# Low fp16 halves of attention weights on GpSimd: every second 512 columns of the long rows, one Trainium2 core

## Chip, cores and metric

The kernel runs on 1 core of one Trainium2 chip. The metric is the device time of one execution in microseconds (us). Before the change the median of 3 runs is 2537.69 us (2535.66 to 2538.88). Engines are named as in the profile: PE is TensorE's matmuls and PEld its weight loads, DVE is VectorE, ACT is ScalarE, POOL is GpSimd, SP is SyncE, whose queue issues the DMAs.

## What is computed

One inference step of a one-layer streaming encoder: an input projection, a short causal convolution, differential attention on 4 heads, an output projection, an MLP and a gated embedding. The attention is what the change touches:

```
u = RMSNorm(h);  z = u @ W_in -> [B | C | X | Q | K | V]
s = einsum('bqhmd,bkhmd->bhmqk', q, k) * HEAD_DIM**-0.5 - slope_h * |t - s|     # two maps m = 0, 1
s = where(chunk(k) <= chunk(q), s, -1e30)
a = softmax(s);  attn = a[:, :, 0] - lam * a[:, :, 1]
o = attn @ v;  o = RMSNorm(o) * (1 - lambda_init)
```

2048 prompt tokens, 64-token chunks, queries in blocks of 128.

## The kernel before

Nearly every matmul is made of three fp16 matmuls: an operand is scaled and split into a high half hi (fp16 of the scaled value) and a low half lo (the scaled value minus hi), and hi*hi, hi*lo and lo*hi are summed in PSUM. `split` (L168) does that with two instructions: ACT writes hi (L170), then DVE writes lo with one scalar_tensor_tensor (L105, through the helper `stt`). `split_in_place` (L173) is another form, used late in the kernel: the source is scaled in place, ACT rounds it to hi, and GpSimd subtracts.

The stages, by the trace: normalised input and first projections (to about 150 us), attention with the other projections woven in (about 150 to 900 us), then the output projection and the MLP's two matrix products, then the embedding gate. The change lies in attention.

Attention goes head by head (j = 0 to 3), and in a head by query blocks of 128 rows; `Unit` is one block. Block qb sees nk = (qb + 1) * 128 keys, taken in pieces of up to 512 columns (`self.chunks`). In heads 0 to 2 qb runs from 0 to 15, in head 3 from 15 down to 0. A unit passes three steps, and `weave` interleaves the steps of three successive units with "fill", generators of projection matmuls and other small work:

- `scores`: two matmuls per piece and map (L617, L618), then on DVE a fused scale, bias and running maximum from PSUM into the fp32 tile s (L621). After the last piece POOL negates the maximum (nm, L100) and ACT takes the exponential of the whole row in place and sums it (L629).
- `weigh` and `turn`, one unit later: POOL and DVE make the two factors r and sg from the row sums. Per piece DVE adds the two maps (L646, into map 0's tile s1), `split` turns the sum into hi and lo, which lie side by side as fp16 in map 1's tile s2 (L647, L648), and one DMA on SP's queue transposes both (L657) into a tile at.
- `values`, another unit later: three 128-column matmuls per 128 keys (L667 to L669) sum into one of four slots of a PSUM tile smb. `subnorm` (L515) then squares the slot on ACT (jko, L518), makes a factor on POOL (rso) and scales on DVE (yg); this also frees the slot.

There are 16 units per head. The units of heads 0 to 2 and the first nine of head 3 (qb 15 to 7) go this way (`by_dma`); the last seven of head 3 use `turn_and_values`, which the change leaves alone. While head 3 ends, `early` splits the output projection's weights (w<-wst, four scaled by i_wo and four by aswo) and starts the first tiles of that projection (L959 to L963).

The order on each engine is fixed when the program is built: a scheduler places the instructions of all engines by their dependencies and its own estimates, in about the order in which they were written. At run time each engine works through its list in that order. SP's DMAs do too. Tile s has four buffers, so two units have rows in flight, and a row's tile is reused when all its readers are done.

Of the kernel before, what the change touches and what calls it, by code (L numbers as in the profile page):

```python
# [11 lines left out]
AF = mybir.ActivationFunctionType  # L12
# [22 lines left out]
def hymba_step_kernel(  # L35
# [9 lines left out]
    V, A, G, T = nc.vector, nc.scalar, nc.gpsimd, nc.tensor  # L45
# [58 lines left out]
    def stt(out, a, s1, b, op0, op1):  # L104
        V.scalar_tensor_tensor(out=out, in0=a, scalar=s1, in1=b, op0=op0, op1=op1)  # L105

    MUL, ADD, SUB, MAX = ALU.mult, ALU.add, ALU.subtract, ALU.max
# [60 lines left out]
    def split(hi, lo, src, scale):  # L168

        A.activation(out=hi, in_=src, func=AF.Copy, scale=scale)  # L170
        stt(lo, src, scale, hi, MUL, SUB)
# [421 lines left out]
    class Unit:  # L593
# [46 lines left out]
        def turn(self):  # L640

            s1, s2 = self.s
            self.ats = []
            for i, (c0, w_) in enumerate(self.chunks):
                cs = slice(c0, c0 + w_)
                stt(s1[:, cs], s2[:, cs], self.r, s1[:, cs], MUL, ADD)  # L646
                hl = s2[:, cs].bitcast(F16)  # L647
                split(hl[:, :w_], hl[:, w_:], s1[:, cs], self.sg)  # L648
                if i < 2 or self.even:
                    if i % 2 == 0:  # L650
                        two = pmix.tile([P, 2, NH, 2, P], F16, tag="q4", bufs=3, name="at2")
                    at = two[:, i % 2].rearrange("p a b c -> p (a b) c")
                else:
                    at = att.tile([P, 2, TG], F16, tag="at", bufs=3, name="at")
                    at = at.rearrange("p a (b c) -> p (a b) c", c=P)
                n = w_ // P
                nc.sync.dma_start_transpose(out=at[:, :2 * n, :], in_=hl)  # L657
                self.ats.append((c0, w_, at[:, :n, :], at[:, n:2 * n, :]))
                yield
# [1127 lines left out]
    for n, (m, p, b) in enumerate(BLOCKS):  # L1787
# [15 lines left out]
        if m == M4 and (p, b) > (0, 1):  # L1803
            i = (4 * p + b - 2) * 2
# [46 lines left out]
```

## Time and profile before

| What | Value |
|---|---|
| Median of 3 runs | 2537.69 us (2535.66 to 2538.88) |
| Profiled execution, its own time | 2533.34 us |
| Its span, first to last instruction | 2531.6 us |
| PE busy | 2456.3 us (97%), 15981 matmuls |
| DVE busy | 1692.4 us (67%), 2931 instructions |
| ACT busy | 1139.1 us (45%) |
| POOL busy | 756.0 us (30%) |
| Mean granted TensorE clock | 0.991 |

Busy shares are averages over stages with different limits, so each stage is read by itself. Matmuls overlap and their ends are modelled, so a busy PE is not a PE at its peak. A wait is put down to what released it last. Idle time on an engine matters only where something else waits for that engine.

### The profile page before, as it was taken

To read this page: it belongs to the slowest core of one execution; us is meant where nothing else is said; L and a number is where in the kernel's file an instruction comes from. 1 tells how busy PE (TensorE), PEld (TensorE's weight loads), DVE (VectorE), ACT (ScalarE), POOL (GpSimd) and SP (SyncE) were. 2 spreads that over 40 slices of the span, in tenths; PEclk is the share of its full clock that TensorE was granted. 3 is DMA by queue.
4 is the path that set the end of the run, shared out by engine and by line. 5 is a ranking of instruction groups with operands and counts; after the bars stand their busy time and mean duration, and the time that the engine had idled before them with its cause. 6 is when DMAs were issued, how large, how long until landed. Compare 5 with 4: busy or idle time off the path is not lost.

```text
span 2531.6 us, 41709 instructions
## 1 busy us (share of the span) xinstructions
PE 2456.3 (97%) x15981; PEld 1283.6 (51%) x15981; DVE 1692.4 (67%) x2931; ACT 1139.1 (45%) x1977; POOL 756.0 (30%) x1307
## 2 busy tenths in 40 slices
PE   8999999999999799999999999999999999999998
PEld 7756655755745444444444444444444444444444
DVE  7578978969988857866665665654455547646664
ACT  5436635635643645643443443454233223425553
POOL 2143344334333434422222222210121102314442
PEclk9999999999999799999999999999999999999999
DMA  5134534524544335454444444366554547631221
GB/s 181 52 84 96 103 81 89 117 61 103 123 104 107 87 120 162 165 209 164 167 160 158 158 175 137 129 243 219 197 193 148 175 152 248 214 96 60 79 84 55
DMA packets 345083, 345.35 MB, mean 136 GB/s; under 512 B 150473, under 2 KB 241042, under 8 KB 344882
## 3 DMA queue, kind: packets, MB, share of 16 engines
q1 hardware_dynamic: 344882, 342.68, 44.4%
q8 instruction: 125, 2.05, 0.3%
q14 instruction: 76, 0.62, 0.1%
HBM read 206.68 MB, written 97.92 MB: 120 GB/s over the span
## 4 chain that ended last, share of the span: by engine, by line
PE 79%; DVE 9%; DMA 5%; ACT 3%; issue 3%; POOL 2%; SPq 0%; DVEq 0%; POOLq 0%; ACTq 0%
PE mm L1383 8%; PE mm L1385 8%; PE mm L1384 8%; PE mm L1614 7%; PE mm L1616 7%; PE mm L1615 7%; PE mm L959 4%; PE mm L961 4%; PE mm L963 4%; PE lin L317 4%; PE lin L318 4%; PE lin L319 4%; DVE s L105 2%; DVE s L621 2%; PE sc L617 1%
## 5 line engine op out<-in xcount | busy, mean ns | idle before, releaser
L1616 PE MATMUL mm<-v,hl 128*128 128x512 f16 x896 | 339.8, 380 | 3.1 <-DVE hl L1576 3.1
L1614 PE MATMUL mm<-v,hl 128*128 128x512 f16 x896 | 339.3, 380 | 2.1 <-ACT hl L1575 2.0
L1615 PE MATMUL mm<-v,hl 128*128 128x512 f16 x896 | 340.3, 380 | 0.0
L317 PE MATMUL lin<-uh,whl 128*128 128x512 f16 (+1 forms) x832 | 261.6, 330 | 4.1 <-DVE yt L105 1.3
L318 PE MATMUL lin<-ul,whl 128*128 128x512 f16 (+1 forms) x832 | 262.2, 330 | 0.7 <-DVE ul L105 0.7
L1576 DVE TENSOR_TENSOR hl<-fr,hl 128x1024 f16<-128x1024 f32 x112 | 150.0, 1349 | 168.1 <-ACT hl L1575 167.2
L319 PE MATMUL lin<-uh,whl 128*128 128x512 f16 (+1 forms) x832 | 261.7, 330 | 0.7 <-DVE whl L105 0.7
L1575 ACT ACTIVATE hl<-fr 128x1024 f16<-128x1024 f32 x112 | 116.7, 1051 | 301.7 <-PE mm L1616 278.2
L629 ACT ACTIVATE s<-s,nm 128x128 f32<-128x128 f32 (+15 forms) x128 | 153.5, 1199 | 167.1 <-POOL nm L100 166.4
L1383 PE MATMUL mm<-u,w 128*128 128x512 f16 x448 | 169.8, 379 | 1.1 <-ACT w L170 1.1
L1384 PE MATMUL mm<-u,w 128*128 128x512 f16 x448 | 169.8, 379 | 0.0
L1384 PE MATMUL mm<-u2b,w 128*128 128x512 f16 x448 | 169.8, 379 | 0.0
L1383 PE MATMUL mm<-u2b,w 128*128 128x512 f16 x448 | 169.2, 379 | 0.5 <-DMA u2b<-u_d 0.5
L1385 PE MATMUL mm<-u,w 128*128 128x512 f16 x448 | 168.8, 379 | 0.0
L1385 PE MATMUL mm<-u2b,w 128*128 128x512 f16 x448 | 168.5, 379 | 0.0
L621 DVE CUSTOM_DVE_ANT_0 s<-sc,bias,mx 128x512 f32<-128x512 f32 (+3 forms) x192 | 134.9, 702 | 16.0 <-PE sc L618 11.8
L1614 PEld LDWEIGHTS <-hl 128*128 128x128 f16 x896 | 87.8, 98 | 112.2 <-issue 6.9
L1616 PEld LDWEIGHTS <-hl 128*128 128x128 f16 x896 | 87.7, 98 | 110.7 <-DVE hl L1576 4.9
L1385 PEld LDWEIGHTS <-w 128*128 128x128 f16 x896 | 87.7, 98 | 105.3
L1615 PEld LDWEIGHTS <-hl 128*128 128x128 f16 x896 | 87.7, 98 | 104.5 <-issue 1.5
L1383 PEld LDWEIGHTS <-w 128*128 128x128 f16 x896 | 88.7, 99 | 100.2 <-ACT w L170 1.2
L1384 PEld LDWEIGHTS <-w 128*128 128x128 f16 x896 | 87.7, 98 | 99.2 <-issue 0.8
(464 smaller groups left out, 5847.8 us busy)
## 6 DMA issues: line engine op xcount, KB each, us to landing
ff_d<-e SPq DMA_DIRECT2D x224, 256.0 KB, 2.1
fr<-ff_d SPq DMA_DIRECT2D x112, 512.0 KB, 4.5
raw<-in_w_down_dram SPq DMA_DIRECT2D x80, 512.0 KB, 4.7
xt<-in_x_prompt_dram SPq DMA_DIRECT2D x32, 512.0 KB, 4.4
stg<-in_w_up_dram SPq DMA_DIRECT2D x16, 1024.0 KB, 6.5
stgd<-in_w_down_dram SPq DMA_DIRECT2D x16, 1024.0 KB, 5.6
stg<-in_w_in_dram SPq DMA_DIRECT2D x24, 512.0 KB, 5.3
h_d<-ht SPq DMA_DIRECT2D x16, 512.0 KB, 2.9
```

Source lines behind the costliest of these rows:

```text
L317: T.matmul(o, w[:, 0, ft], rh[:, ft, c], start=(ft == 0), stop=False)
L318: T.matmul(o, w[:, 0, ft], rl[:, ft, c], start=False, stop=False)
L319: T.matmul(o, w[:, 1, ft], rh[:, ft, c], start=False, stop=(ft == FT - 1))
L621: ev = V.tensor_tensor_reduce(out=s_[:, c0:c0 + w_], in0=ps[:, :w_], in1=bias[:, b0:b0 + w_], scale=h["idd"], scalar=-BIG if prev is None ...
L629: A.activation(out=s_[:, :nk], in_=s_[:, :nk], func=AF.Exp, bias=nm, accum_out=zz)
L1383: T.matmul(o, w[:, c, 0, kt], x[:, :, 0, kt], start=first and kt == 0, stop=False, skip_group_check=True)
L1384: T.matmul(o, w[:, c, 0, kt], x[:, :, 1, kt], start=False, stop=False, skip_group_check=True)
L1385: T.matmul(o, w[:, c, 1, kt], x[:, :, 0, kt], start=False, stop=kt == 3, skip_group_check=True)
L1576: V.tensor_tensor(out=hl[:, 1], in0=fr, in1=hl[:, 0], op=SUB)
L1614: T.matmul(ps, hl[:, 0, u % 2, c], v[:, 0], start=(u == 0), stop=False)
L1615: T.matmul(ps, hl[:, 0, u % 2, c], v[:, 1], start=False, stop=False)
L1616: T.matmul(ps, hl[:, 1, u % 2, c], v[:, 0], start=False, stop=(u == NU - 1))
```

## The change

In `turn`, for the pieces with odd index (i = 1 and 3) of the blocks with qb > 7, `split` is replaced by three instructions: ACT multiplies the sum by sg in place, ACT copies it to hi, and GpSimd subtracts hi from the scaled sum into lo. Other pieces and blocks keep `split`.

```diff
                 stt(s1[:, cs], s2[:, cs], self.r, s1[:, cs], MUL, ADD)
                 hl = s2[:, cs].bitcast(F16)
-                split(hl[:, :w_], hl[:, w_:], s1[:, cs], self.sg)
+                if i % 2 and self.qb > 7:
+                    A.activation(out=s1[:, cs], in_=s1[:, cs], func=AF.Copy, scale=self.sg)
+                    A.copy(hl[:, :w_], s1[:, cs])
+                    G.tensor_tensor(out=hl[:, w_:], in0=s1[:, cs], in1=hl[:, :w_], op=SUB)
+                else:
+                    split(hl[:, :w_], hl[:, w_:], s1[:, cs], self.sg)
```

Per head the odd pieces are: i = 1 with 512 columns in the eight blocks qb 8 to 15, and i = 3 in qb 12 to 15 with 128, 256, 384 and 512 columns. That is 12 pieces a head and 48 in all, 36 of 512 columns and 4 each of 384, 256 and 128. In the changed program the three new instructions are lines L649 (scale), L650 (copy, printed as CAST) and L651 (subtract).

The scheduler's order moves with them. In the lists below s_N are row tiles (N is the tile's number, which differs between the two programs), sc the PSUM scores, mx a running maximum, sgc, sg, ca, kk and rz the small factors of a unit.

On DVE, in head 0, the row with qb 12, around the low halves of its pieces. Before:

```order
L621 ISA s_4076,mx<-sc,bias,idd_1557 128x512
L621 ISA mx 128x1
L105 SCALAR_TENSOR_TENSOR s_3847<-s_3786,sg,s_3847 128x512
L140 TENSOR_REDUCE am<-stg 128x1
L105 SCALAR_TENSOR_TENSOR s_3847<-s_3786,sg,s_3847 128x512 x2
L105 SCALAR_TENSOR_TENSOR s_3847<-s_3786,sg,s_3847 128x128
L621 ISA s_4076,mx<-sc,bias,mx,idd_1557 128x512
L621 ISA mx 128x1
```

and now:

```order
L105 SCALAR_TENSOR_TENSOR s_3850<-s_3789,sg,s_3850 128x512
L100 TENSOR_SCALAR yg<-smb,rso 128x128
L105 SCALAR_TENSOR_TENSOR s_3850<-s_3789,sg,s_3850 128x512
L621 ISA s_4080,mx<-sc,bias,mx,idd_1557 128x512
L621 ISA mx 128x1
L621 ISA s_4080,mx<-sc,bias,mx,idd_1557 128x512
L621 ISA mx 128x1
```

The low halves of pieces 1 and 3 are gone from DVE's list; those of pieces 0 and 2 stay, and behind them stand steps of the scores of a later row.

On POOL, at the same row of head 0. Before:

```order
L102 TENSOR_SCALAR rso<-sso,kk 128x1
L102 TENSOR_SCALAR kk<-sg,z_3808,k_0_1759 128x1
L521 TENSOR_TENSOR rso<-rso,mhalf 128x1
L102 TENSOR_SCALAR kk<-kk 128x1
L100 TENSOR_SCALAR nm<-mx 128x1 x2
L102 TENSOR_SCALAR ca<-z_4037,alam,z_4134 128x1
```

and now:

```order
L102 TENSOR_SCALAR rso<-sso,kk 128x1
L521 TENSOR_TENSOR rso<-rso,mhalf 128x1
L100 TENSOR_SCALAR nm<-mx 128x1
L651 TENSOR_TENSOR s_3850<-s_3789,s_3850 128x512
L651 TENSOR_TENSOR s_3850<-s_3789,s_3850 128x128
L100 TENSOR_SCALAR nm<-mx 128x1
L102 TENSOR_SCALAR ca<-z_4041,alam,z_4138 128x1
```

Two subtractions now stand between two negated maxima (nm), and the second nm follows both.

On ACT, near the end of head 3, at the splitting of the output projection's weights. Before:

```order
L170 ACTIVATE yhl<-pty,gsa 128x4x128
L170 ACTIVATE w<-wst,i_wo 128x1024 x4
L629 ACTIVATE s_12357,z_12369<-s_12357,nm 128x1024
L170 ACTIVATE w<-wst,aswo 128x1024 x4
L518 ACTIVATE jko,sso<-smb 128x128
L170 ACTIVATE s_12282<-s_12250,sg 128x512 x2
L170 ACTIVATE s_12282<-s_12250,sg 128x128
L629 ACTIVATE s_12372,z_12396<-s_12372,nm 128x1024
```

and now:

```order
L170 ACTIVATE yhl<-pty,gsa 128x4x128
L170 ACTIVATE w<-wst,i_wo 128x1024 x4
L170 ACTIVATE w<-wst,aswo 128x1024 x4
L629 ACTIVATE s_12404,z_12416<-s_12404,nm 128x1024
L170 ACTIVATE s_12328<-s_12296,sg 128x512
L649 ACTIVATE s_12296<-s_12296,sg 128x512
L170 ACTIVATE s_12328<-s_12296,sg 128x128
L518 ACTIVATE jko,sso<-smb 128x128
L629 ACTIVATE s_12419,z_12443<-s_12419,nm 128x1024
```

The exponential of the row with qb 7 has moved behind all eight weight halves, and jko now follows the three instructions that turn pieces 0 to 2 of the row with qb 8, where it stood ahead of that row's pieces; the copy of its piece 1 comes after the last row shown.

## Rows read from the trace of the kernel before

**Rows 1.** Windows by stage: us, busy us (instructions) per engine, granted clock, DMA share, GB/s.
```profile
150.00:820.00 670.00, 649.01 (x5416) 388.79 (x5415) 564.92 (x1370) 346.01 (x647) 269.04 (x607) 1.00 0.45 98
820.00:900.00 80.00, 60.45 (x396) 35.80 (x395) 61.78 (x144) 48.75 (x105) 36.55 (x95) 0.83 0.33 85
...
1030.00:1650.00 620.00, 618.34 (x3570) 288.32 (x3569) 390.62 (x562) 263.07 (x437) 170.21 (x170) 1.00 0.47 162
```

**Rows 2.** Windows of the four long-row stretches, same columns, with their sum.
```profile
222.00:322.00 100.00, 96.33 (x1041) 67.52 (x1040) 89.86 (x221) 60.68 (x107) 39.40 (x85) 1.00 0.53 110
412.00:502.00 90.00, 86.21 (x943) 62.37 (x943) 81.55 (x193) 59.22 (x107) 33.96 (x75) 0.98 0.54 109
612.00:700.00 88.00, 82.20 (x905) 58.50 (x903) 80.99 (x191) 56.10 (x95) 28.65 (x63) 1.00 0.55 117
700.00:826.00 126.00, 118.21 (x812) 62.27 (x810) 104.65 (x246) 54.46 (x91) 44.68 (x85) 0.99 0.45 104
sum 404.00, PE 382.95 PEld 250.66 DVE 357.04 ACT 230.46 POOL 146.69; mean PE 95.74 PEld 62.66 DVE 89.26 ACT 57.61 POOL 36.67
```

**Rows 3.** Waits of PE, 150 to 820 us: total us, times, longest.
```profile
PE smb L667 <- DMA at<-s: 6.5, 9, 1.1
PE sc L617 <- DVE mx L621: 5.5, 10, 1.0
```

**Rows 4.** Groups of DVE, 150 to 820 us: shapes, count | busy us, mean ns | idle.
```profile
L105 DVE SCALAR_TENSOR_TENSOR s<-s,sg,s 128x512 f16<-128x512 f32 x102 | 73.1, 741 | 6.8 <-ACT s L170 6.7
...
L105 DVE SCALAR_TENSOR_TENSOR s<-s,sg,s 128x384 f16<-128x384 f32 x14 | 8.5, 608 | 1.6 <-ACT s L170 1.6
...
L105 DVE SCALAR_TENSOR_TENSOR s<-s,sg,s 128x256 f16<-128x256 f32 x13 | 6.2, 477 | 1.2 <-ACT s L170 1.2
...
L105 DVE SCALAR_TENSOR_TENSOR s<-s,sg,s 128x128 f16<-128x128 f32 x13 | 4.5, 343 | 0.0
```

**Rows 5.** Groups of ACT, 150 to 820 us, same columns.
```profile
L170 ACT ACTIVATE s<-s,sg 128x512 f16<-128x512 f32 x102 | 68.5, 714 | 61.7 <-DVE s L105 38.0 <-POOL sg L102 21.9 <-POOL kk L102 1.3
```

**Rows 6.** Groups of POOL, 1030 to 1650 us, same columns.
```profile
L1274 POOL TENSOR_TENSOR stg<-stg 128x512 f32<-128x512 f32 x16 | 28.0, 1749 | 14.1 <-DVE w L105 14.1
...
L1267 POOL TENSOR_TENSOR s3t<-stg 128x512 f32<-128x512 f32 x15 | 19.1, 1271 | 141.7 <-DMA stg<-in_w_up_dram 141.7
```

**Rows 7.** Line L105, a DVE helper: min/median/max ns, first and last start, forms.
```profile
L105 DVE SCALAR_TENSOR_TENSOR w<-stg,i_u,w x96: 734/741/1767, 1033.3 to 1637.5; 128x512 f16<-128x512 f32 x96
...
L105 DVE SCALAR_TENSOR_TENSOR e<-mm,sr,e x64: 733/744/753, 1076.8 to 1678.7; 128x512 f32<-128x512 f32 x64
```

**Rows 8.** Timelines of POOL, then DVE, 1632 to 1635 us: start, us, instruction.
```profile
1632.61 1.79 POOL L1274 TENSOR_TENSOR stg<-stg 128x512 f32<-128x512 f32 x1
...
1633.18 1.75 DVE L105 SCALAR_TENSOR_TENSOR w<-s3t,i_u,w 128x512 f16<-128x512 f32 x1
1634.86 0.74 DVE L105 SCALAR_TENSOR_TENSOR w<-stg,i_u,w 128x512 f16<-128x512 f32 x1
```

**Rows 9.** Line L657, the transposing DMAs: min/median/max ns, first and last start.
```profile
L657 SPq DMA_TRANSPOSE at<-s x150: 1181/1258/2643, 156.4 to 849.1; - x150
```

**Rows 10.** Waits of all engines, 150 to 820 us.
```profile
ACT s L629 <- POOL nm L100: 151.2, 70, 6.3
```

**Rows 11.** Timelines of ACT, then PE, around 830 to 842 us.
```profile
830.01 4.26 ACT L170 ACTIVATE w<-wst,i_wo 128x1024 f16<-128x1024 f32 x4 [0.42 <-DVE i_wo L102]
834.18 1.13 ACT L629 ACTIVATE s<-s,nm 128x1024 f32<-128x1024 f32 x1
...
835.31 4.25 ACT L170 ACTIVATE w<-wst,aswo 128x1024 f16<-128x1024 f32 x4
839.47 0.26 ACT L518 ACTIVATE jko<-smb 128x128 f16<-128x128 f32 x1
...
839.72 1.62 ACT L170 ACTIVATE s<-s,sg 128x512 f16<-128x512 f32 x3
...
841.53 0.27 PE L667 MATMUL smb<-vhl,at 128*128 128x128 f16 x1 [6.04 <-DVE yg L100]
```

## The prediction

> **What bounds the kernel now.** I read the windows by stage first. From 150 to 820 us, where attention runs with fill, PE is busy 649.01 of 670 us, DVE 564.92, ACT 346.01 and POOL 269.04; in the MLP stretch from 1030 to 1650 us PE is busy 618.34 of 620 [rows 1]. So attention is bound by PE with DVE close behind, and POOL and ACT have room. At its end, 820 to 900 us, PE is busy only 60.45 of 80 us at a granted clock of 0.83 [rows 1]: the fill is used up, and a chain through the engines sets the pace.
>
> Then I cut out the parts that hold the changed rows, which are four long-row stretches. Together they last 404 us; PE is busy 382.95 and DVE 357.04, that is 88% [rows 2]. PE's idle time there is 404 - 382.95 = 21.05 us. This is all that an easier DVE could give back in these stretches, since the matmuls stay the same. The list of PE's waits says for what it stands: from 150 to 820 us 6.5 us in 9 waits for the transposed weights at, and 5.5 us in 10 waits for a score buffer that DVE must empty [rows 3]. Both can come from a late DVE, but no wait is longer than 1.1 us.
>
> **What leaves DVE.** 48 low halves go: 36 of 512 columns at 741 ns, and 4 each of 384, 256 and 128 columns at 608, 477 and 343 ns [rows 4]. That is 36 * 0.741 + 4 * (0.608 + 0.477 + 0.343) = 26.7 + 5.7 = 32.4 us, 9% of DVE's 357.04 us.
>
> **What POOL's subtraction gives back to DVE.** A subtraction of 512 columns in fp32 takes POOL 1271 ns in one group and 1749 ns in another [rows 6]. The difference is in what DVE does at the same moment. In the timeline POOL's subtraction runs from 1632.61 for 1.79 us; DVE's low half, which reads two SBUF tiles, starts inside it and takes 1.75 us, while the next one, behind it, takes 0.74 [rows 8]. The same form ranges from 734 to 1767 ns over that stage, but one that has a PSUM operand stays between 733 and 753 [rows 7]. So a subtraction can cost a DVE instruction with two SBUF tiles 1.75 - 0.74 = 1.01 us, more than the 0.741 us it saved, and those with a PSUM operand nothing.
>
> How often they meet isn't in the trace of before. By the order on DVE, the score steps that follow the low halves of pieces 0 and 2 read PSUM and the bias tile, so most subtractions should run beside these. I take one in three, 16 * 1.01 = 16.2 us, and 32.4 - 16.2 = 16.2 us remain as relief for DVE. The bounds are none (32.4 us of relief) and all (48 * 1.01 = 48.5, a loss of 16.1 us).
>
> The Trainium skill, SBUF — State Buffer, section "Who interferes with whom", describes this as an exclusive lock: GpSimd reading SBUF and a VectorE instruction with two SBUF inputs exclude each other for a whole instruction, and the loser waits. This speaks against the change; the stretched 1.75 us beside 0.74 agrees with it, and so does the form with a PSUM operand. By that rule alone the sum would still depend on how often they meet; that it is always is a rival below.
>
> **Term 1, PE's idle time in the long rows: -6 us.** The relief of 16.2 us is half of what DVE was freed of. PE can't gain more than the 21.05 us. The waits in the list that DVE can be behind sum to 6.5 + 5.5 = 12.0 us, and I take half of these. Bounds: 0 and -21.
>
> **Term 2, later transposes: +3 us.** The new chain of a changed piece is scale, copy, subtract instead of hi, lo. ACT has one instruction more, priced at the 714 ns of hi [rows 5] (a write of fp32 in place isn't among the rows; its nearest row is this one, with the same source and size). POOL's 1.27 to 1.75 replaces 0.741. So the piece is 0.714 + 1.27 - 0.741 = 1.24 us later, up to 0.714 + 1.75 - 0.741 = 1.72, before any queueing. What waits behind it: SP's queue, where the transposing DMA (1258 ns each, 150 of them [rows 9]) waits for the subtraction and later DMAs wait behind that one; and POOL's own queue, in which a negated maximum follows two subtractions in the order shown, while ACT already waits 151.2 us in 70 places for that value [rows 10]. ACT has time, and PE has fill. So I count only the places where PE takes the weights as soon as they land: 9 of 150 transposes now, hence some 3 of 48, each 1.24 us later, 3.7 us; I take 3. Bounds: 0, and 12 of 48 at 1.72, or 21 us.
>
> ACT's own addition, 48 instructions of at most 0.714 us (34 us), I put at nothing: it is spread over 404 us in which ACT is busy 230.46 [rows 2]. POOL's, at most 48 * 1.75 = 84 us, fits beside its 146.69 too. Without that cover they would show as term 2.
>
> **Term 3, the chain at the end: +2 us.** Around 830 us ACT splits the output weights, 4.26 and 4.25 us with an exponential of 1.13 between; jko starts at 839.47 only then, and PE has stood 6.04 us for the slot that jko's chain frees [rows 11]. In the new order the exponential stands behind all eight halves and jko also behind two of 512 columns and one of 128. The three of that size that used to follow took 1.62 us in all [rows 11]. The exponential was ahead of jko before as well, so jko comes about 1.6 us later, and PE's wait of 6.04 us grows by it, since no fill is left. I take 2 for what hangs on it. Bounds: 0, if the scheduler's other moves there make up for it, and +5, if the next slot is late by the same again and the copy of piece 1 adds POOL's 1.75 us.
>
> **The sum** is made against the profiled execution, 2533.34 us (span 2531.6): -6 + 3 + 2 = -1, so 2532.3 us. The median of the runs, 2537.69, lies 4.35 us above that execution, and I forecast a median: 2532.3 + 4.35 = 2536.7 us. A measurement of this kernel can tell about 0.2%, 5.1 us, from no change, so this is no change, and its own range is 2532.6 to 2542.8.
>
> **Rivals.**
>
> *DVE was the real bound of the long rows.* For it: 88% busy, and a static order in which every late low half delays the next scores. Against: no wait of PE exceeds 1.1 us, and fill stands ready. If no subtraction meets a two-tile instruction, all 32.4 us of relief count and two thirds of PE's 21.05 us idle go: -14 + 1 + 2 = -11, or 2526.7 us. Chance 0.30.
>
> *Weights come late to PE (the slower side).* The place is the first product (L667) of pieces 1 and 3: SP and POOL work strictly in order, so one late copy on ACT holds the subtraction, the transpose and the maxima behind it. For it: two subtractions ahead of a maximum, and the 9 waits of today. Against: ACT turns pieces 0 and 2 while the pair is made, and pieces are used a unit later. If 12 of 48 are late by 1.5 us, that is +18, with -8 of DVE's relief and +2 at the end +12, or 2549.7 us; it decides the sign from about 8 late pieces. Chance 0.17.
>
> *Every subtraction meets a two-tile instruction.* Then DVE has 16.1 us more work instead of 32.4 less, 373 of 404 us; PE's idle time grows by a third of that, 5, and with terms 2 and 3 the sum is +10: 2547.7 us. For it: row sums (L646) and weight halves read two tiles. Against: the order beside the subtractions. Chance 0.08. This is the lock of the Trainium skill's SBUF page in its full weight.
>
> That the change isn't made as described is excluded by the order: 48 low halves less on DVE, 48 subtractions more on POOL.
>
> **Chances and range.** My forecast has 0.42, the faster rival 0.30 and the two slower ones 0.25 together; 0.03 more I give to a term 1 between forecast and rival that just passes 0.2%. So faster 0.33, same 0.42, slower 0.25. For 8 in 10 the range must take in the faster rival with some room and most of the slower ones: 2525 to 2549.
>
> **What would show it.** DVE's groups: low halves of 512 columns down by 36, and 32 us less there. POOL: 48 subtractions with a mean between 1.27 and 1.75 us; the nearer to 1.75, the more they meet. The row sums and remaining low halves would rise above 741 ns where they meet. PE's idle time in the four stretches: 21.05 now, about 18 forecast with terms 1 and 2. PE's waits for at: 6.5 us now, about 9 forecast; over 20 would be the late-weights rival. The wait at the slot near 835 us: 6.04 now, 7 to 8 forecast. Wrong it would be if PE's idle in the stretches fell under 12 us, or if the stages after 900 us, whose instructions stay, moved by more than 2 us.

## The result, and the profile after

The changed kernel takes 2559.49 us (median of 4 runs, 2559.22 to 2559.84), the kernel before 2538.05 us in the same comparison: 1.0091 times as long, 95% interval 1.0079 to 1.0103. That is about 23 us slower (0.0091 * 2538; the medians differ by 21.4, which is inside the interval). Forecast was 1 us faster, and the range ended at 2549.

The page of the changed kernel, its first part:

```profile
span 2557.7 us, 41838 instructions
PE 2467.5 (96%) x15981; PEld 1287.4 (50%) x15981; DVE 1681.7 (66%) x2883; ACT 1158.4 (45%) x2025; POOL 794.5 (31%) x1355
```

Against the table ahead of the prediction the profiled span has grown by 26.1 us (that execution of the kernel before lay 4.7 us under its median): PE's busy time by 11.2 us (2456.3 to 2467.5) and its idle time by 14.9, at a mean granted clock of 0.987 instead of 0.991. DVE, which the change was to relieve, has 48 instructions less, but only 10.7 us less busy time (1692.4 to 1681.7) instead of 32.4. Where most of the rest went stands in the groups from 150 to 840 us of DVE, then POOL, then ACT (columns as in rows 4):

```profile
L105 DVE SCALAR_TENSOR_TENSOR s<-s,sg,s 128x512 f16<-128x512 f32 x68 | 62.0, 923 | 9.4 <-ACT s L170 9.3
...
L651 POOL TENSOR_TENSOR s<-s,s 128x512 f16<-128x512 f32 x34 | 43.0, 1268 | 36.2 <-ACT s L650 36.1
...
L649 ACT ACTIVATE s<-s,sg 128x512 f32<-128x512 f32 x34 | 24.1, 709 | 0.8 <-DVE s L105 0.8
L650 ACT CAST s<-s 128x512 f16<-128x512 f32 x34 | 20.4, 605 | 0.1
```

The remaining low halves of 512 columns take 923 ns on average instead of 741 [rows 4], 12.4 us more for the 68. At 1.01 us for a full meeting [rows 8] that is as much as 12 full meetings; 16 were forecast. (A run below that frees DVE in the same way, without any subtraction, lowers DVE's busy time by 27.5 us, 1692.4 to 1664.9; so some 5 us of what is missing here are not the subtraction's.) The subtraction keeps its short time of 1268 ns on average, and the scale in place takes 709 ns (the estimate was 714).

The long rows last longer now. For about the same work, from 216 us on and cut where PE does the same thing in both kernels, the windows of before are

```profile
216.00:330.00 114.00, 110.33 (x1154) 75.82 (x1153) 99.13 (x243) 69.47 (x131) 46.65 (x104) 1.00 0.47 98
420.00:518.00 98.00, 94.21 (x1015) 67.37 (x1014) 79.04 (x187) 57.53 (x108) 33.59 (x76) 0.98 0.50 101
602.00:701.00 99.00, 93.20 (x978) 64.17 (x976) 91.54 (x214) 61.51 (x105) 32.66 (x74) 1.00 0.53 113
701.00:757.00 56.00, 53.47 (x362) 27.81 (x361) 46.58 (x110) 28.13 (x48) 21.99 (x38) 1.00 0.47 104
```

and those of the changed kernel

```profile
216.00:337.00 121.00, 112.70 (x1156) 77.39 (x1154) 97.75 (x234) 76.70 (x145) 56.59 (x117) 0.99 0.46 94
427.00:529.00 102.00, 95.17 (x1025) 67.28 (x1023) 85.33 (x197) 65.69 (x126) 49.06 (x97) 1.00 0.52 103
611.00:714.00 103.00, 94.83 (x968) 64.22 (x967) 90.76 (x206) 65.80 (x117) 46.85 (x86) 0.98 0.52 112
714.00:776.00 62.00, 57.36 (x373) 30.64 (x372) 46.42 (x108) 33.01 (x56) 22.29 (x46) 0.94 0.47 98
```

Together they grow from 367 to 388 us: 7 us in head 0, 4 in head 1, 4 in head 2, 6 in the first rows of head 3. (2 us come back between the second and the third, where 84 us become 82.) The granted clock (third column from the end) falls to 0.94 in the first rows of head 3. PE's idle time in these four is 15.8 us before and 27.9 now. The other 9 us are PE's busy time; a part of them is the clock, and these windows of the changed kernel also hold 13 matmuls more. At the end, where term 3 lay, the long wait for the slot is 1.9 us longer (below). The waits from 150 to 820 us (rows 3 and 10 have those of before):

```profile
PE sc L617 <- DVE mx L621: 13.0, 15, 2.7
PE smb L672 <- DMA at<-s: 7.5, 8, 1.5
...
ACT s L629 <- POOL nm L100: 164.6, 69, 6.5
...
POOL s L651 <- ACT s L650: 39.9, 26, 5.1
```

Late weights are hardly there (7.5 us against 6.5). What grew is PE's wait for a score buffer that DVE empties, from 5.5 to 13.0 us, with single waits of up to 2.7 us where none was over 1.0. On a DVE with less to do, that needed experiments.

### The profile page after: what moved, and what is told of

It reads as the page before. It is cut to its first block, busy times and chain, and to the rows that moved or that the text cites. A ratio compares the mean times of both kernels' runs of the same rounds, so it can differ in the third digit from the quotient of the medians.

```text
span 2557.7 us, 41838 instructions
## 1 busy us (share of the span) xinstructions
PE 2467.5 (96%) x15981; PEld 1287.4 (50%) x15981; DVE 1681.7 (66%) x2883; ACT 1158.4 (45%) x2025; POOL 794.5 (31%) x1355
## 4 chain that ended last, share of the span: by engine, by line
PE 70%; DVE 12%; DMA 5%; ACT 5%; issue 4%; POOL 3%; SPq 0%; DVEq 0%; POOLq 0%; ACTq 0%
PE mm L1388 8%; PE mm L1390 7%; PE mm L1389 7%; PE mm L1619 6%; PE mm L1621 6%; PE mm L1620 6%; PE mm L964 4%; PE mm L966 4%; PE mm L968 4%; DVE s L621 3%; DVE s L105 3%; PE lin L317 2%; PE lin L319 2%; PE lin L318 2%; ACT s L629 2%
## 5 line engine op out<-in xcount | busy, mean ns | idle before, releaser
L319 PE MATMUL lin<-uh,whl 128*128 128x512 f16 (+1 forms) x832 | 261.5, 330 | 0.7 <-DVE whl L105 0.7
L1388 PE MATMUL mm<-u,w 128*128 128x512 f16 x448 | 170.3, 380 | 1.1 <-ACT w L170 1.1
L1388 PE MATMUL mm<-u2b,w 128*128 128x512 f16 x448 | 169.2, 379 | 0.1
L1388 PEld LDWEIGHTS <-w 128*128 128x128 f16 x896 | 88.9, 99 | 100.7 <-ACT w L170 1.2
```

The source lines that it names most:

```text
L319: T.matmul(o, w[:, 1, ft], rh[:, ft, c], start=False, stop=(ft == FT - 1))
L1388: T.matmul(o, w[:, c, 0, kt], x[:, :, 0, kt], start=first and kt == 0, stop=False, skip_group_check=True)
```

## The experiments

**Work and order apart.** The change does two things at once: it gives the engines other instructions, and the scheduler then writes other lists for all of them. Edges that only fix the order of issue can hold a given list. This function, called after the whole program is traced, does it. `d`, unpacked from the text `ORDER`, holds for each instruction by how many places it must move to stand as in the other kernel's common list (a cut; "..." marks what is left out):

```
for _, i in sorted(((n + x, i) for n, (x, i) in enumerate(zip(d, ins))), key=lambda p: p[0]):
    e = str(i.engine).split(".")[-1]
    ...
    if e in last:
        tc.add_manual_dep(i, last[e].name,
                          mybir.DependencyInfo(mybir.DependencyClass.NoSync, mybir.DependencyReason.DATA), reason="hold")
    last[e] = i
```

"Old order" is the list of the kernel before on every engine, "new order" that of the changed kernel; PE's and SP's lists are then word for word the same as there (in the traces PE's 15981 matmuls follow each other as there in every such run). First the new work in the old order, and the old work in the new:

> The three new instructions of each of the 48 pieces, but every engine's list is held in the order of the kernel before by edges between neighbours: scale and copy stand where hi stood on ACT, the subtraction stands on POOL where the scheduler's common list had DVE's low half, and everything else keeps its place. Theory A (the work itself: a longer chain scale, copy, subtract, and POOL's strict queue make weights and maxima late): the cost stays, 2555 to 2564 us. Theory B (the order: the scheduler, fed with other instructions, wrote other lists for PE, DVE, ACT and SP, and those lists are the slower ones): the cost goes, 2530 to 2541 us, and what is left of DVE's relief may show as a few us under 2538. Theory C (POOL's subtraction stretches DVE's low halves, 923 ns mean against 741): it would stay with the old order as well, some 12 us of DVE time, 2543 to 2552 us.

Measured: 2551.16 us, 1.0053 (1.0041 to 1.0066).

> The mirror of the run above: the instructions of the kernel before (ACT writes hi, DVE writes lo), but every engine's list is held in the order of the changed kernel: hi stands where the copy stood on ACT, lo stands on DVE where the common list had POOL's subtraction. Theory A (the work): 2536 to 2543 us. Theory B (the order): 2554 to 2564 us, or above that, since DVE has the 32 us of low halves on top. Theory C (the stretching): 2536 to 2543 us, as no POOL subtraction is left in attention.

Measured: 2570.12 us, 1.0135 (1.0117 to 1.0154). No theory alone fits both: the first run is in theory C's range and in no other, and the second is above all of them but B's. The new work costs some 13 us in the old order, and the new order is bad for the old work too. The second run probably overstates it, since DVE's low half stands at POOL's late place there. So I took work that fits in both orders without choosing a place: ACT writes both halves, so that the low half is a copy of the high one.

```
-                    A.copy(hl[:, :w_], s1[:, cs])
-                    G.tensor_tensor(out=hl[:, w_:], in0=s1[:, cs], in1=hl[:, :w_], op=SUB)
+                    A.activation(out=hl[:, w_:], in_=s1[:, cs], func=AF.Copy, scale=self.sg)
```

(This is a cut, against the changed kernel; the scale then writes hi, in `hl[:, :w_]`, instead of working in place.)

> Lists held in the order of the kernel before. DVE's 48 low halves are taken away and POOL gets nothing: ACT writes the high half twice, the second time into the low half's place (the output is then not the reference's, since the low half of these pieces is wrong). That is DVE's whole relief of 32 us, with as many ACT instructions as in the change. If DVE's time were worth something in this order, 2527 to 2534; if PE's list bounds it and DVE had room, 2536 to 2540; if ACT's extra instruction alone costs (theory A1), 2543 or more.

Measured: 2535.67 us, 0.9998 (0.9989 to 1.0007). **DVE's whole relief and ACT's second instruction come to nothing together**: -0.5 us, by the interval between 3 us faster and 2 slower. That each is worth nothing, and that the two do not cancel, no run shows by itself; PE's waits speak for it (from 150 to 820 us 6.1 us for scores and 6.1 for weights, 5.5 and 6.5 before).

> The instructions of the run in which ACT writes the high half twice (48 low halves gone from DVE, nothing on POOL; the low half of these pieces is wrong), this time with every list held in the order of the changed kernel: the first write stands where the scale stood on ACT, the second where the copy stood, and PE, DVE and SP have word for word the changed kernel's lists, POOL too but for the 48 subtractions. In the old order this work took 2535.7 us. Theory B (the new lists themselves are slower): 2550 to 2559, and the step from there to the changed kernel's 2559.5 is the price of the subtraction in its own order. If the new lists are no worse (theory A), 2536 to 2543.

Measured: 2545.19 us, 1.0033 (1.0020 to 1.0046). **The new lists alone cost 0.0035 * 2538, about 9 us.** And the way from there to the changed kernel is 0.0091 - 0.0033 = 0.0058, about 15 us, as in the old order: 0.0053 + 0.0002 = 0.0055, about 14. Within the intervals, some 3 to 5 us on each such difference, the two causes add up.

Where most of the order's 9 us lie shows at once in the windows from 720 to 750 us of the two runs in which ACT writes both halves. In the old order:

```profile
720.00:730.00 10.00, 7.98 (x40) 3.27 (x38) 9.00 (x23) 7.88 (x13) 3.59 (x10) 1.00 0.75 186
730.00:740.00 10.00, 10.00 (x72) 5.65 (x71) 7.39 (x22) 8.65 (x15) 4.54 (x8) 1.00 0.24 46
740.00:750.00 10.00, 10.00 (x85) 5.75 (x83) 6.48 (x13) 5.12 (x10) 3.98 (x7) 1.00 0.47 108
```

and in the new order:

```profile
720.00:730.00 10.00, 7.07 (x34) 2.98 (x32) 7.69 (x17) 5.66 (x8) 1.69 (x2) 0.95 0.65 171
730.00:740.00 10.00, 7.45 (x27) 2.98 (x26) 8.65 (x24) 7.21 (x13) 4.93 (x12) 0.67 0.21 40
740.00:750.00 10.00, 10.00 (x71) 6.46 (x70) 7.87 (x21) 8.88 (x15) 3.22 (x7) 0.87 0.68 100
```

PE idles 5.5 us instead of 2.0, and the granted clock falls to 0.67 and 0.87 after it: 17.45 us of matmuls at these clocks lose by estimate 7.45 * 0.33 + 10 * 0.13 = 3.8 us. With the idle time that makes 7.2 of the 9. The list says why. Between the last fill matmul (L319) and the first product (L667 before, L672 now) PE's list holds score matmuls with little else between. Here are the first of each pair (the second, L618, follows each). Before:

```
L617 MATMUL sc<-ks_9173,qs 128x512
L617 MATMUL sc<-ks_9173,qs 128x384
L617 MATMUL sc<-ks_9172,qs 128x512
L617 MATMUL sc<-ks_9172,qs 128x512
L617 MATMUL sc<-ks_9172,qs 128x512
L617 MATMUL sc<-ks_9172,qs 128x256
L617 MATMUL sc<-ks_9173,qs 128x512
```

and in the changed kernel:

```
L617 MATMUL sc<-ks_9198,qs 128x384
L617 MATMUL sc<-ks_9197,qs 128x512
L617 MATMUL sc<-ks_9197,qs 128x512
L617 MATMUL sc<-ks_9197,qs 128x512
L617 MATMUL sc<-ks_9197,qs 128x256
L617 MATMUL sc<-ks_9198,qs 128x512
L617 MATMUL sc<-ks_9198,qs 128x512
L617 MATMUL sc<-ks_9198,qs 128x512
L617 MATMUL sc<-ks_9198,qs 128x256
L617 MATMUL sc<-ks_9197,qs 128x512
```

Ten pairs in a row instead of seven; the products that could stand between come after. A pair of 512 columns takes PE 0.43 us (two starts of the timeline apart), and DVE takes 0.8 us to empty its buffer, with other work between. So PE must wait, and does so in the timeline of the changed kernel, DVE first, then PE:

```profile
747.08 2.59 DVE L105 SCALAR_TENSOR_TENSOR s<-s,sgc,s 128x512 f32<-128x512 f32 x4
749.59 0.81 DVE L621 CUSTOM_DVE_ANT_0 s<-sc,bias,mx 128x512 f32<-128x512 f32 x1
...
742.26 0.38 PE L617 MATMUL sc<-ks,qs 128*128 128x512 f16 x1 [1.90 <-DVE mx L621]
...
744.80 0.63 PE L617 MATMUL sc<-ks,qs 128*128 128x512 f16 x1
...
750.46 0.41 PE L617 MATMUL sc<-ks,qs 128*128 128x512 f16 x1 [2.74 <-DVE mx L621]
```

Four additions of the two maps (L646, through the helper L105) stand on DVE ahead of the maximum for which PE waits 2.74 us, and between the waits PE's matmul takes 0.63 us instead of 0.38.

**What an order is worth by itself.** One number of the kernel before is changed, which moves fill steps and no work:

```
-    NFILL = {0: 62, 1: 95, 2: 92, 3: 94}
+    NFILL = {0: 61, 1: 95, 2: 92, 3: 94}
```

> The kernel before with one number changed that moves no work between engines: head 0 is given 61 instead of 62 steps of fill while its blocks run. The scheduler then writes another order for head 0 and what follows (1861 of PE's rows stand elsewhere). It says what an order is worth without any change of work. Theory B (orders of the same work differ by as much as the change): it differs from before by 5 us or more, either way. Theory A: within 3 us of 2538.

Measured: 2547.01 us, 1.0035 (1.0019 to 1.0051).

> A second order of the same work: the kernel before with 94 instead of 95 fill steps in head 1. Theory B (the order alone is worth as much as this change): it is 4 us or more away from 2538, as the first such run was with +10. If the first was an accident: within 3 us.

Measured: 2537.50 us, 1.0009 (1.0000 to 1.0019).

> A third order of the same work: the kernel before with 63 instead of 62 fill steps in head 0. Expectations as for the second.

Measured: 2542.09 us, 1.0021 (1.0012 to 1.0030). Three other orders of the same work cost 9, 2 and 5 us, the 2 within what was expected of an accident and with an interval that reaches down to nothing; none gains. As far as three orders tell, a change that makes the scheduler write a new order is likelier to start with a loss than with a gain. The changed kernel with 61 fill steps in head 0:

> The changed kernel with 61 instead of 62 fill steps in head 0, so with other lists and the same work. By the runs so far the work costs some 13 to 15 us in either order, and three other orders of the old work cost 2 to 10. So 2546 to 2562; nearer to 2551 it would say that the changed kernel's own order is one of the worse ones, nearer to 2560 that it is an ordinary one.

Measured: 2559.65 us, 1.0096 (1.0081 to 1.0112). So its own order is no worse than this other one.

**The 14 us of the work.** All further runs hold the old order. ACT's part alone has `V.tensor_tensor` in place of `G.tensor_tensor` in the changed lines:

> Lists held in the order of the kernel before. Only ACT's part of the change: it scales in place and copies, and the subtraction stays on DVE, at the place of the old low half. PE's, POOL's and SP's lists are those of before. The run with all three new instructions in that order took 2551.2 us, 12.8 above before. If ACT's extra 0.7 us a piece makes the weights late (theory A1), most of the 12.8 stays: 2547 to 2552. If POOL does it, by its longer subtraction, its strict queue or the stretching of DVE (theory A2), it goes: 2536 to 2542.

Measured: 2544.89 us, 1.0036 (1.0023 to 1.0050), between the two theories. The same number of ACT instructions cost nothing when ACT wrote both halves; with the low half a step later, and on DVE, they cost 9 us. How, its profile doesn't show: DVE waits only 1.2 us for these copies (150 to 840 us), and against the run in which ACT writes both halves PE's idle time grows by 2.6 us (74.5 to 77.1), its busy time by 7.9 (2458.0 to 2465.9), at a mean granted clock of 0.987 instead of 0.989. POOL's part alone:

```
+                    A.activation(out=hl[:, :w_], in_=s1[:, cs], func=AF.Copy, scale=self.sg)
+                    G.tensor_tensor(out=hl[:, w_:], in0=hl[:, :w_], in1=hl[:, :w_], op=SUB)
```

> Lists held in the order of the kernel before. Only POOL's part: ACT writes hi with the scale in one instruction as before, and POOL subtracts hi from itself into the low half's place (the low half of these pieces is then zero and the output not the reference's; POOL reads fp16 instead of fp32). Theory A2 (POOL's longer subtraction, its queue, the stretching of DVE's halves): 2545 to 2552. Theory A1 (ACT's extra instruction): 2536 to 2541.

Measured: 2543.12 us, 1.0022 (1.0012 to 1.0032). This is under the expected 2545, but clearly not nothing. So both parts cost, and theories A1 and A2 each have a part in it. POOL's can act in two ways: by making the weights late, or by what it does on POOL and to DVE. The next run takes the first away; ACT writes both halves, and then

```
+                    G.tensor_tensor(out=s1[:, cs], in0=s1[:, cs], in1=hl[:, :w_], op=SUB)
```

> Lists held in the order of the kernel before, as in the run in which ACT writes the high half twice (2535.7 us), and POOL gets its 48 subtractions back at the same places of its list, but into the dead row sum, so that no transpose waits for them (the low half of these pieces stays wrong). POOL's queue is as full, its reads are the same, and DVE's two-tile instructions are stretched where they meet; only the chain to the transposed weights is short. If the cost of the subtraction is its place in the chain (theory D: weights late), 2535 to 2538. If it is the stretching of DVE or POOL's strict queue (theory C), 2541 to 2550.

Measured: 2544.62 us, 1.0035 (1.0022 to 1.0048), 9 us over the same work without POOL. No transpose waits for these subtractions. What is left is POOL's strict queue or the meeting with DVE:

```
-                    G.tensor_tensor(out=s1[:, cs], in0=s1[:, cs], in1=hl[:, :w_], op=SUB)
+                    G.tensor_tensor(out=s1[:, c0:c0 + 1], in0=s1[:, c0:c0 + 1], in1=hl[:, 0:1], op=SUB)
```

> As the run with the subtraction beside the chain (2544.6 us in the old order, 2535.7 without POOL's part), but each subtraction is cut to one column: POOL's strict queue still waits at the same 48 places until ACT has written hi, but works there for about 0.3 us instead of 1.2 and hardly reads SBUF. If the wait in POOL's strict queue is the cost (theory E: the maxima and factors behind it come late), 2541 to 2546. If it is the meeting with DVE's two-tile instructions or POOL's busy time (theory C), 2535 to 2539.

Measured: 2538.56 us, 1.0004 (0.9995 to 1.0013).

> As the run above, with three one-column subtractions instead of one at each place: POOL waits for hi and is then busy for about a microsecond, much as with 512 columns, but reads almost nothing that could stretch DVE's instructions. Theory C in its narrow form (the stretching of DVE's halves is the cost): 2535 to 2539 like the run above. If POOL's busy time in its strict queue is the cost: 2541 to 2546, while the one-column run is lower.

Measured: 2537.45 us, 0.9998 (0.9989 to 1.0006). Three one-column subtractions turned out to keep POOL for only 3 * 0.19 = 0.6 us, half of the 1.16 of the full ones, so the busy time was tested by half. These are the medians (second of the three times) of their lines, small and full:

```profile
L652 POOL TENSOR_TENSOR s<-s,s x144: 181/192/1558, 222.8 to 844.9; 128x1 f32<-128x1 f32 x144
...
L651 POOL TENSOR_TENSOR s<-s,s x48: 422/1158/1550, 221.0 to 847.1; 128x512 f32<-128x512 f32 x36, 128x128 f32<-128x128 f32 x4, 128x256 f32<-128x256 f32 x4, 128x384 f32<-128x384 f32 x4
```

POOL's wait for ACT was the same or longer, and costs nothing. Among DVE's costly groups from 150 to 840 us only the low halves differ by more than 1 us. With one column:

```profile
L105 DVE SCALAR_TENSOR_TENSOR s<-s,sg,s 128x512 f16<-128x512 f32 x69 | 50.8, 743 | 8.2 <-ACT s L170 8.0
```

and with the full subtraction beside the chain:

```profile
L105 DVE SCALAR_TENSOR_TENSOR s<-s,sg,s 128x512 f16<-128x512 f32 x69 | 59.2, 865 | 7.9 <-ACT s L170 7.5
```

One such meeting, in the timeline of the run with the full subtraction beside the chain (POOL, then DVE):

```profile
259.42 1.23 POOL L651 TENSOR_TENSOR s<-s,s 128x512 f32<-128x512 f32 x1 [0.88 <-ACT s L650]
260.63 0.64 POOL L100 TENSOR_SCALAR nm<-mx 128x1 f32<-128x1 f32 x1
...
258.89 0.75 DVE L105 SCALAR_TENSOR_TENSOR s<-s,sg,s 128x512 f16<-128x512 f32 x1
259.98 1.22 DVE L105 SCALAR_TENSOR_TENSOR s<-s,sg,s 128x512 f16<-128x512 f32 x1 [0.34 <-ACT s L170]
261.12 0.80 DVE L621 CUSTOM_DVE_ANT_0 s<-sc,bias,mx 128x512 f32<-128x512 f32 x1
```

The first low half starts 0.53 us before the subtraction and takes 0.75 us. The second starts inside the subtraction, ends 0.55 us after it and takes 1.22; the next score step follows. So 8 to 9 us of the kernel hang on what one column takes away: the stretching of 8 us of DVE time, or POOL's full busy time, which is not quite excluded. ACT's wait for POOL's maxima, through which it would act, doesn't tell (150 to 820 us): 150.8 us here, 145.1 with the three small ones, 141.2 without any, but 151.2 in the kernel before. How the stretching reaches PE is open: PE's waits for scores and weights there sum to 12.2 us, as much as without the subtraction.

**A step that the prediction pointed to.** Term 3 read that jko stands behind ACT's eight weight halves. In the kernel before, 18 instructions of ACT change places, and nothing else:

```
-  w x4 (i_wo), exp 1024, w x4 (aswo), jko, hi x3, exp 1024, hi x2, jko, exp 896
+  exp 1024, jko, hi x3, w x4 (i_wo), exp 1024, hi x2, jko, exp 896, w x4 (aswo)
```

> The kernel before, with its own lists on all engines but for 18 instructions of ACT near 830 us: the eight output weight halves, which stood ahead of jko, are moved behind it: the exponential of 1024 columns, jko and the three halves of the row come first, then four weight halves, then the next row's five instructions, then the other four. If term 3 of the prediction has read that wait rightly (PE stands 6.04 us for a slot that jko frees, and jko stands behind ACT's weight halves), PE's wait falls to under 2 us and the kernel takes 2531 to 2536 us. If other waits at the end take over, 2536 to 2539.

Measured: 2532.94 us, 0.9987 (0.9977 to 0.9996), **3.3 us faster than the kernel before**, and the only run that beats both. Timelines of ACT, then PE, in its profile:

```profile
830.50 0.28 ACT L518 ACTIVATE jko<-smb 128x128 f16<-128x128 f32 x1 [0.51 <-PE smb L669]
...
832.88 4.25 ACT L170 ACTIVATE w<-wst,i_wo 128x1024 f16<-128x1024 f32 x4
...
835.33 0.22 PE L667 MATMUL smb<-vhl,at 128*128 128x128 f16 x1 [1.43 <-DVE yg L100]
```

PE's wait of 6.04 us [rows 11] is 1.43 now. From 820 to 900 us its waits for slots fall from 8.8 to 4.0 us, while those for scores rise from 7.9 to 10.1, so a part of the gain is taken by the next wait.

## Why the prediction was wrong

Three steps failed: the worth of DVE's relief in term 1 (-6 us forecast, -0.5 measured), the price of the subtraction, which was only set off against that relief (+9), and the order of the lists, which got no term (+9). By the old and the new order together the parts are, in ratios times 2538 us: relief of DVE -0.5 (0.9998), order +8.9 (1.0033 - 0.9998), meetings +9.4 (1.0035 - 0.9998), later chain +4.6 (1.0053 - 1.0035, by the intervals 0 to 9). The sum is 22.4 us, and 23 were measured by the ratio, 21.4 by the medians. The division between meetings and chain depends on the order in which they are added: with POOL's part alone in the chain it is 6 and 8 us (1.0022 - 0.9998, and 1.0053 - 1.0022).

**Term 1 failed in kind.** "Half of PE's waits" was to go when DVE has 16 us less to do. With 32 us less on DVE and only a second write on ACT in their place, the time did not change. A reason that fits, argued and not shown: the waits in rows 3 are for one late instruction each, and an instruction that leaves DVE shortens one of them only if it stood just ahead of the late one. The rival "DVE was the real bound" falls with it: where no subtraction met DVE and all 32 us counted, its 88% were no limit.

**What the subtraction gives back was counted about rightly and priced wrongly.** DVE lost 12.4 us to them in the low halves of 512 columns, where 16.2 were forecast. But I subtracted them from the relief, as if DVE's microseconds were one currency. The freed ones were worth nothing; the lost ones, which stand ahead of scores and of the next weights, cost about their full length in one run (9.4 us of time for 8.4 us of stretched halves beside the chain) and less in another (POOL's part alone: 6 us for 69 * (0.884 - 0.743) = 9.7). That freed and lost time differ by what stands behind them is argued from the timelines, not shown by a run. The rule of the Trainium skill that was quoted (SBUF — State Buffer, section "Who interferes with whom") agrees with the 1.22 us beside 0.75 in the timeline of the meeting, though there the half's record ends only 0.55 us after the subtraction's, not its whole 0.75 (spans on POOL are rough). The one-column runs, in which POOL waits and reads nearly nothing, take the cost away. The rival "every subtraction meets" had the right mechanism, but priced 48 meetings at 5 us of PE's idle time (10 with terms 2 and 3); a quarter of these meetings, as full ones, was enough for 9.

**Term 2 had the right sign, and its size is open.** 3 us were forecast; 5 fit, with 0 to 9 by the intervals, and ACT's part alone took 9. In the old order PE's waits for weights (150 to 820 us) show the later chain, first beside it and then in it:

```profile
PE smb L672 <- DMA at<-s: 7.7, 13, 1.1
...
PE smb L672 <- DMA at<-s: 10.2, 17, 2.3
```

In the changed kernel they are 7.5 us, where over 20 was the sign of the rival "weights come late"; that rival falls. ACT's additional instruction at nothing held when ACT wrote both halves.

**Term 3 read its wait rightly.** jko comes behind the exponential and the three moved instructions, and PE waits 7.94 us instead of 6.04, where 7 to 8 were forecast. What it costs is less sure: of the three waits for slots at the end two shorter ones are gone, so that they sum to 7.9 us now and 8.8 before; from the last L319 matmul on `lin` to the first of the MLP (L1383, now L1388) it is 252.4 us instead of 251.1. In the changed kernel's timelines of ACT, then PE:

```profile
852.64 4.25 ACT L170 ACTIVATE w<-wst,aswo 128x1024 f16<-128x1024 f32 x4
856.79 1.14 ACT L629 ACTIVATE s<-s,nm 128x1024 f32<-128x1024 f32 x1
...
859.44 0.26 ACT L518 ACTIVATE jko<-smb 128x128 f16<-128x128 f32 x1
...
861.25 0.26 PE L672 MATMUL smb<-vhl,at 128*128 128x128 f16 x1 [7.94 <-DVE yg L100]
```

**The step that was missing.** I read the new order at the changed instructions and at the end, and took the rest of the lists as equal. Some 7 of the order's 9 us lie in the first rows of head 3, on PE's list, in which no instruction was changed. The sentence "since the matmuls stay the same" was true of their number and not of their order. The list was there to be read ahead: ten pairs of scores in a row, at 0.43 us each on PE and 0.8 on DVE, leave PE some 10 * (0.8 - 0.43) = 3.7 us short even if DVE does nothing else. But the seven of before leave 2.6 by the same estimate, so it would have given the place and not the size. The clock, which made it worse, was in rows 1 (0.83 at the end), and I gave it no term.

**The sign after 900 us.** The prediction was to be wrong if the stages after 900 us moved by more than 2 us, and in the profiled executions they did: the MLP's second product lasts 4.3 us longer. One of its three matmul lines before, changed, and with ACT writing both halves in the old order (min/median/max ns, first and last start in us):

```profile
L1614 PE MATMUL mm<-v,hl x896: 376/379/634, 1669.6 to 2288.9; 128*128 128x512 f16 x180
...
L1619 PE MATMUL mm<-v,hl x896: 378/379/631, 1691.5 to 2315.1; 128*128 128x512 f16 x180
...
L1618 PE MATMUL mm<-v,hl x896: 378/379/634, 1666.8 to 2289.9; 128*128 128x512 f16 x180
```

The last of these takes 623.1 us, nearly as long as the changed kernel's 623.6 and longer than the 619.3 of before, in a run whose time did not change. So this much lies between executions and says nothing of the change.

## What to carry to other kernels

Where a scheduler writes the lists, compare the whole list of the bounding engine before and after, above all for runs of instructions that one other engine must serve, and measure work and order apart by holding the order. Relief of an engine that is not the bound can be worth nothing (32 us of DVE here), while a stretch of the same engine can cost about as much time as it lasts (9 us for 8 in one run, 6 for 10 in another). So don't set one against the other.

## What the runs showed of the hardware

TensorE's granted clock went down to the lower of its two levels (1.2 instead of 2.4 GHz) beside waits of 1.9 to 2.7 us on PE. In the changed kernel it is 0.51 from 743.8 to 747.3 us, after a wait of 1.90 us, and a matmul of 128x512 takes 0.63 us instead of 0.38 at 744.80 us. In the run with ACT's two writes in the new order, with waits of 1.93 and 2.55 us, it is 0.67 on average from 730 to 740 us. In the old order, with waits of at most 0.7 us, the same stretch stayed at 1.00. The prediction counted waits at their length; in this stretch the clock took about as much again (3.8 us, an estimate, beside 3.5 of more idle time).

A GpSimd subtraction of 512 columns from SBUF drew out VectorE's low halves, which read two SBUF tiles: 1.22 us instead of 0.75 in the timeline, 865 ns on average instead of 743, while the score step, which reads PSUM and one SBUF tile, kept its 802 ns. Cut to one column, the subtraction left the low halves at 743 ns.
